# Neighbourhood attention with the meta keys in the right strip's unused column, and a new order of the splits at the up stage's border

## The chip, the cores and the metric

The kernel runs on one core of a Trainium2 chip. The metric is the device time of one execution in microseconds (us); the median of three runs before the change is 1512.63 us (1512.05 to 1513.26).

## The reference

One layer of an encoder on 16 meta tokens and 1024 real tokens of width 1024, in float32. The real tokens form a grid of 16 rows and 64 columns.

```
a = rms_norm(h, g)
q_na, k_na, v_na, q_hg, z_f, z_b, i_hg, g_hg, gate_na, gate_hg = split(a @ W_in)
A  = neighbourhood_attention(q_na, k_na, v_na, rpb) @ W_na      # 8 heads of 64
Bm = hgrn2(q_hg, z_f, z_b, i_hg, g_hg) @ W_hg                   # 4 heads of 128
h  = h + (sigmoid(gate_na) * A + sigmoid(gate_hg) * Bm) @ W_o
h  = h + square(relu(rms_norm(h) @ W_up)) @ W_down              # 4096 wide
out = rms_norm(h)[16:]
```

In the attention a query at row r, column c sees 8 rows and 16 columns (both clamped at the grid's borders; in the middle the columns c-8 to c+7) with a bias by relative place, and all 16 meta keys. One softmax runs over the 128 + 16 scores.

## The kernel before

**Precision.** Every large product is made of float32r matmuls: each operand is split into a high part (a rounding copy, on ACT) and a low part (a subtraction, on DVE), and three matmuls, high x high, high x low and low x high, are added up in PSUM (`mm3`, L121; `chain`, L913: twelve matmuls of 512 columns over four blocks of 128). Transposes are plain float32 matmuls with the identity.

**Stages in order of time.** Projections and the gated recurrence (to about 340 us); the attention, head pair by head pair (about 340 to 580); the gates, the two branch outputs, W_o; the up product; the down product. Where nothing is said, a planner orders the instructions of all engines by program order as priority and by a model of costs. Where `manual_schedule` is open for an engine, program order is its order.

**The attention** (L749 to L899), for each of four pairs of heads. The 64 columns are cut into 8 strips of 8 columns; a strip has 16 x 8 = 128 tokens. Queries stand in `QX`, keys in `KS` (high part) and `KL` (low part), each strip of keys followed by the 16 meta keys, SW = 144 columns in all. Inside a strip tokens run row by row, so that the evictions of the projections (`ev_k`, L790; `ev_vn`, L810) write runs. `mev_k` (L799) puts the meta keys behind all eight strips.

`scores` (L831): for one strip and one head two matmuls (high and low keys) over the strips left, centre and right with their meta columns: 432 columns inside, 288 at the two edges. DVE adds bias and mask from `NB` and takes the minimum (L844), ACT makes the exponential and its sum (L846), DVE takes the reciprocal (L847) and scales (L848). A mask lets the meta columns count only once, behind the centre strip.

`values` (L851): each of the m strips of probabilities is transposed (L859), and once more the 128 columns that end with the meta columns of the centre (L861), so that the 16 meta probabilities stand in the last 16 rows of that block. ACT and DVE split the block into PH and PL (L870, L871). After four strips come the products with V, whose blocks hold 64 columns of the high and 64 of the low part: first the meta block V[:, 8] against the four meta blocks of PH, 512 columns (L875), then for each strip of keys one matmul with PH (L882) and one of the high part with PL (L883), as wide as the strips of queries that see it, last V[:, 8] against PL, 512 columns (L884). V[:, 8] is zero but for its last 16 rows. V's nine blocks come out of nine transposes of `vT` (L821) and a split (L823, L824).

The steps run in the order: four strips of head 0, four of head 1, then the other half; `values` lags `scores` by two steps. While that goes on the planner lets PE stream the projections of the next pair. `NB` is built on POOL (L774) from a bias and a mask that SP loads.

**The border to the up product** (L1278 to L1506). The rows of h, 128 at a time in `hres[0..7]`, get their W_o product, are written to DRAM (`row_scale`, L1231, on ACT's queue), scaled (`scale_row`, L1242), transposed back into place (`turn_back`, L1271), and combined two by two into the variants of a seven-product (Strassen-like) scheme: `row_sums` (L1245, two subtractions on DVE, two on POOL) gives t1, t2, t3, t4 and b22, and `split_rows(v, j)` (L1287, `to_variant` L1258) splits one block of one variant: one ACT copy and one DVE subtraction (L1261, L1262). From L1462 to the loop's end the order of all engines is written out by hand. The list `todo` holds the splits that are still open. For the first three pairs of column blocks of w_up the products with b11 and b21 (`product_1`, `product_2`) are made ahead, while row 7 and the splits are being finished; their weights are split by `weights` (L1323, ACT L1328, DVE L1329). Then the loop over the pairs runs products 3 to 7 with s4, s2, s1, s3, a22, the split sums of w_up's blocks (`pair_sums`, L1371).

## Time and profile before

| what | value |
|---|---|
| median of three runs | 1512.63 us |
| the profiled execution | 1511.24 us |
| its span, first to last instruction | 1509.5 us |
| granted TensorE clock | 0.999 |
| PE busy | 1492.1 us |
| DVE, ACT, POOL busy | 1035.8, 665.0, 370.7 us |

The span is that of one profiled execution. A row of a group gives the line, the engine, the operation, the tiles as out<-in with the shapes and the count; behind the bar the busy time in us and the mean of one in ns; behind the second bar the idle time of the engine just ahead of them and what ended it. A PE row with 128*128 128x512 has 128 x 128 weights and 512 moving columns. PEld rows are the loads of the weights, which overlap PE. PE's durations are latencies of a pipeline: in a timeline, starts tell the pace.

### The profile page before, as it was taken

Reading aid. Unit: us, or ns where it says so; the run is one execution under the profiler, and the core shown is the slowest. Engines: PE = TensorE matmul, PEld = TensorE weight load, DVE = VectorE, ACT = ScalarE, POOL = GpSimd, SP = SyncE. Lnnn points to the kernel's source line nnn. Section 1 sums busy time; section 2 is a strip of 40 time slices with the busy share of each in tenths; the row PEclk is TensorE's granted clock in tenths of the full one; section 3 lists DMA queues with packets and bytes.
Section 4 is the critical chain, followed back from the end, with each engine's and each line's share of the span. In section 5 each row is a group of like instructions: output and inputs, shape, how many; then the busy total and the mean of one; then the engine's idle time right before and its main releaser. Section 6 shows DMA issues by size and latency. Waiting matters only on the chain.

```text
span 1509.5 us, 23492 instructions
## 1 busy us (share of the span) xinstructions
PE 1492.1 (99%) x9200; PEld 1250.8 (83%) x9200; DVE 1035.8 (69%) x1622; ACT 665.0 (44%) x1185; POOL 370.7 (25%) x349
## 2 busy tenths in 40 slices
PE   9999999999999999999999999999999999999998
PEld 8888888888888888888888878888888888888886
DVE  7876666656786796675585478777777445877876
ACT  7131313135565576343133355555555534334444
POOL 3313131324414400110000131344444200231242
PEclk9999999999999999999999999999999999999999
DMA  4211011114212237444655124544444676563224
GB/s 170 59 30 57 29 50 37 44 30 132 87 63 95 98 91 259 140 152 168 223 169 209 42 91 167 168 154 154 154 154 153 203 252 234 189 233 112 96 84 154
DMA packets 142592, 195.62 MB, mean 130 GB/s; under 512 B 8192, under 2 KB 90368, under 8 KB 142480
## 3 DMA queue, kind: packets, MB, share of 16 engines
q1 hardware_dynamic: 133072, 172.34, 34.8%
q10 hardware_dynamic: 7232, 14.44, 2.5%
q0 software_dynamic: 2176, 7.34, 1.3%
q8 instruction: 72, 1.18, 0.3%
q14 instruction: 40, 0.33, 0.1%
HBM read 139.56 MB, written 54.53 MB: 129 GB/s over the span
## 4 chain that ended last, share of the span: by engine, by line
PE 92%; DVE 4%; issue 2%; ACT 2%; POOL 0%; DMA 0%; POOLq 0%; ACTq 0%; DVEq 0%
PE mm L122 11%; PE mm L123 11%; PE mm L124 11%; PE mm L1541 5%; PE pa L1541 5%; PE pb L918 4%; PE pb L919 4%; PE pb L920 4%; PE pb L1541 4%; PE pc L1541 4%; PE pc L920 3%; PE pc L919 3%; PE pc L918 3%; PE pa L920 2%; PE pa L919 2%
## 5 line engine op out<-in xcount | busy, mean ns | idle before, releaser
L122 PE MATMUL mm<-aT,hi 128*128 128x512 f32 (+2 forms) x600 | 213.9, 357 | 0.0
L123 PE MATMUL mm<-aT,hi 128*128 128x512 f32 (+2 forms) x600 | 211.9, 353 | 0.0
L124 PE MATMUL mm<-aT,lo 128*128 128x512 f32 (+2 forms) x600 | 211.7, 353 | 0.0
L96 ACT CAST dh<-ur 128x1024 fp32r<-128x1024 f32 x54 | 56.9, 1054 | 166.5 <-issue 91.1
L97 DVE TENSOR_TENSOR dl<-ur,dh 128x1024 fp32r<-128x1024 f32 x54 | 70.0, 1297 | 87.0 <-ACT dh L96 85.2
L122 PEld LDWEIGHTS mm<-aT,hi 128*128 128x128 f32 x600 | 113.2, 189 | 12.6
L124 PEld LDWEIGHTS mm<-aT,lo 128*128 128x128 f32 x600 | 113.2, 189 | 12.3
L123 PEld LDWEIGHTS mm<-aT,hi 128*128 128x128 f32 x600 | 113.3, 189 | 12.0
L1333 ACT ACTIVATE uv<-uv 128x512 f32<-128x512 f32 x48 | 30.4, 633 | 82.3 <-DVE uv L1441 52.8
L1329 DVE TENSOR_TENSOR wl<-sx,wh 128x512 fp32r<-128x512 f32 x70 | 62.1, 897 | 3.6 <-ACT wh L1328 3.6
L1329 DVE TENSOR_TENSOR wl<-raw,wh 128x512 fp32r<-128x512 f32 x50 | 39.0, 783 | 36.4 <-ACT wh L1328 36.3
L112 ACT CAST hi<-raw 128x1024 fp32r<-128x1024 f32 x26 | 27.3, 1052 | 77.1 <-PE mm L123 71.3
L1328 ACT CAST wh<-sx 128x512 fp32r<-128x512 f32 x70 | 42.3, 620 | 38.5 <-PE pc L919 24.8
L1631 POOL TENSOR_TENSOR w<-w,tt 128x512 f32<-128x512 f32 x16 | 24.3, 1521 | 132.3 <-DVE tt L1630 111.1
L844 DVE CUSTOM_DVE_ANT_0 pr<-nsc,NB 128x432 f32<-128x432 f32 (+1 forms) x64 | 35.3, 560 | 30.2 <-issue 22.9
L300 POOL TENSOR_TENSOR Y<-X,TN 128x512 f32<-128x512 f32 x20 | 34.2, 1711 | 83.4 <-DVE X L297 83.4
L122 PE MATMUL mm<-wh,mT 128*128 128x512 f32 x128 | 50.2, 392 | 0.0
L123 PE MATMUL mm<-wl,mT 128*128 128x512 f32 x128 | 50.1, 391 | 0.0
L124 PE MATMUL mm<-o,lo 128*128 128x512 f32 x128 | 49.9, 390 | 0.1
L918 PE MATMUL pb<-nt,wh 128*128 128x512 f32 x128 | 49.9, 390 | 0.0
L124 PE MATMUL mm<-wh,mT 128*128 128x512 f32 x128 | 49.9, 390 | 0.0
L123 PE MATMUL mm<-o,hi 128*128 128x512 f32 x128 | 49.8, 389 | 0.0
(432 smaller groups left out, 4425.3 us busy)
## 6 DMA issues: line engine op xcount, KB each, us to landing
raw<-in_w_in SPq DMA_DIRECT2D x56, 512.0 KB, 3.9
ur<-usp SPq DMA_DIRECT2D x54, 512.0 KB, 3.6
raw<-in_w_up SPq DMA_DIRECT2D x16, 1024.0 KB, 6.2
usp<-us SPq DMA_DIRECT2D x60, 256.0 KB, 2.4
sg<-gsp SPq DMA_DIRECT2D x16, 512.0 KB, 5.1
w<-in_w_dn SPq DMA_DIRECT2D x16, 512.0 KB, 5.0
usp<-uv SPq DMA_DIRECT2D x30, 256.0 KB, 2.3
gsp<-gv ACTq DMA_DIRECT2D x24, 256.0 KB, 2.4
```

What stands on the lines that cost most here:

```text
L96: act.copy(hi, src)
L97: dve.tensor_tensor(lo, src, hi.bitcast(F32), op=ALU.subtract)
L122: pe.matmul(ps, lh, rh, start=first, stop=False)
L123: pe.matmul(ps, lh, rl, start=False, stop=False)
L124: pe.matmul(ps, ll, rh, start=False, stop=last)
L844: dve.tensor_tensor_reduce(out=pr[:, :w], in0=sc[:, :w], in1=NB[:, i, o:o + w], scale=1.0, scalar=3.0e38, op0=ALU.add, op1=ALU.min, accum_ ...
L918: pe.matmul(ps, lhs[0][:, c], rhs[0][:, k], start=first and k == 0, stop=False, skip_group_check=True)
L919: pe.matmul(ps, lhs[0][:, c], rhs[1][:, k], start=False, stop=False, skip_group_check=True)
L920: pe.matmul(ps, lhs[1][:, c], rhs[0][:, k], start=False, stop=k == 3, skip_group_check=True)
L1328: act.copy(v(hi), src)
L1329: dve.tensor_tensor(v(lo), src, v(hi).bitcast(F32), op=ALU.subtract)
L1541: pe.matmul(ps, a[n == 2][:, q, j * P:(j + 1) * P], b[n == 1][:, q], start=first and n == 0, stop=last and n == 2, skip_group_check=True)
```

## The change

**Attention.** The tokens of a key strip run column by column, with the 16 meta keys ahead of them. Seen from its query strip, the last column of the right strip never lies in the window; so the right strip is read from its start, 16 meta keys and seven columns, 128 in all, and an inner strip's scores are 3 x 128 columns: two matmuls of 256 and two of 128. The two edge strips keep two matmuls of 288. The probabilities are transposed in three blocks of 128 everywhere. V gets 14 blocks: eight whole strips, and six (strips 2 to 7) that begin with the meta values; they take 14 transposes in four batches. The 512-column meta products are gone; a right strip is a matmul of its own with its own V block, and only each half's edge strip has a meta product left, over 16 rows. Bias and mask are laid out accordingly on the host.

**Border.** Four of the row tiles (`hres` 2, 6, 3, 7) move to a pool of their own, `hrb`, whose slots later hold w_up's split weights in place of the pool `upr`. The first half of the third pair's weights is split ahead of row 7's scaling, from `upf`, which gets two buffers. Row 7's spill goes to SP's queue. The last `row_sums` runs on DVE alone. The splits of t3 and t4 for blocks 2 and 3 are put off: two to the place ahead of pair 2's product 2, one behind the next weights, one behind the first product 6; the remaining ones move between the products.

```diff
-        vT = npl.tile([P, 9, P], F32, name="vT")
-        V = npr.tile([P, 9, 2, P], F32R, name="Vn")
+        def key_strips(t, p0, t0, n):
+
+            a = t[p0:p0 + 64, :, NM:].rearrange("p s (c r) -> p s r c", r=ROWS)
+            return a[:, :, t0 // 64:(t0 + n) // 64]
...
-                    act.copy(strips(KS[i], 64 * i, t0, n), grid(ps, 64 * i))
+                    act.copy(key_strips(KS[i], 64 * i, t0, n), grid(ps, 64 * i))
...
-                    dve.tensor_tensor(strips(KL[i], b, t0, n), grid(ps, b),
-                                      strips(KS[i], b, t0, n).bitcast(F32), op=ALU.subtract)
-                    act.copy(strips(KS[i], 64 - b, t0, n), strips(KS[i], b, t0, n).bitcast(F32))
+                    dve.tensor_tensor(key_strips(KL[i], b, t0, n), grid(ps, b),
+                                      key_strips(KS[i], b, t0, n).bitcast(F32), op=ALU.subtract)
+                    act.copy(key_strips(KS[i], 64 - b, t0, n), key_strips(KS[i], b, t0, n).bitcast(F32))
...
             def mev_vn(ps):
-                act.copy(vT[:, 8, P - NM:], ps)
+                act.copy(vT[:, :, :NM], ps.unsqueeze(1).broadcast_to([P, 8, NM]))
             proj(C_VN + p * P, ev_vn, mev_vn)
-            for b in (0, 4, 8):
+            whole = [vT[:, j, NM:] for j in range(8)] + [vT[:, j, :P] for j in range(2, 8)]
+            for b in range(0, len(whole), 4):
...
             def scores(s, i):
-                js = [j for j in (s - 1, s, s + 1) if 0 <= j < 8]
-                w = len(js) * SW
-                o = 432 if s == 0 else 720 if s == 7 else 0
-                sc = bank("s", "nsc").rearrange("p a b -> p (a b)")
-                ksl = KS[i][:, js[0]:js[-1] + 1].rearrange("p s c -> p (s c)")
-                kll = KL[i][:, js[0]:js[-1] + 1].rearrange("p s c -> p (s c)")
-                pe.matmul(sc[:, :w], QX[i][:, s], ksl, start=True, stop=False)
-                pe.matmul(sc[:, :w], QX[i][:, s], kll, start=False, stop=True)
-                pr = npr.tile([P, 432], F32, tag="pr", name="pr", bufs=5)
+                sc = bank("s", "nsc")
+                scf = sc.rearrange("p a b -> p (a b)")
+                if 0 < s < 7:
+                    w, o = 3 * P, 0
+                    runs = [(sc[:, :2], [K[i][:, s - 1:s + 1, NM:] for K in (KS, KL)]),
+                            (sc[:, 2], [K[i][:, s + 1, :P] for K in (KS, KL)])]
+                else:
+                    w, o = 2 * SW, 3 * P + (2 * SW if s else 0)
+                    j = max(s - 1, 0)
+                    runs = [(scf[:, :w], [K[i][:, j:j + 2].rearrange("p s c -> p (s c)") for K in (KS, KL)])]
+                for dst, (ks, kl) in runs:
+                    pe.matmul(dst, QX[i][:, s], ks, start=True, stop=False)
+                    pe.matmul(dst, QX[i][:, s], kl, start=False, stop=True)
+                sc = scf
+                pr = npr.tile([P, 3 * P], F32, tag="pr", name="pr", bufs=5)
...
-                    po[i] = [npr.tile([P, 22, P], F32R, tag=f"PT{q}", name=f"PT{q}") for q in range(2)]
+                    po[i] = [npr.tile([P, 19, P], F32R, tag=f"PT{q}", name=f"PT{q}") for q in range(2)]
...
-                for k in range(m):
-                    pe.transpose(pt[:, k], pr[:, k * SW:k * SW + P], ident)
-                cen = js.index(s)
-                pe.transpose(pt[:, m], pr[:, cen * SW + NM:cen * SW + NM + P], ident)
-
-                b0 = 3 * (js[0] - 4 * g) + e + 3
-                if s < 7:
-                    runs = [(0, m + 1, b0)]
-                else:
-                    runs = [(0, m, b0), (m, 1, 4 * e + 9)]
-                for k, n, b in runs:
-                    hi = PH[:, b:b + 3 * n - 2:3]
-                    act.copy(hi, pt[:, k:k + n])
-                    dve.tensor_tensor(PL[:, b:b + 3 * n - 2:3], pt[:, k:k + n], hi.bitcast(F32), op=ALU.subtract)
+                for k, c in enumerate((0, P, 2 * P) if 0 < s < 7 else (NM, SW + NM, SW)):
+                    pe.transpose(pt[:, k], pr[:, c:c + P], ident)
+                b0 = 3 * (max(s - 1, 0) - 4 * g) + e + 3
+                hi = PH[:, b0:b0 + 7:3]
+                act.copy(hi, pt[:, :3])
+                dve.tensor_tensor(PL[:, b0:b0 + 7:3], pt[:, :3], hi.bitcast(F32), op=ALU.subtract)
...
-                pe.matmul(ov, V[:, 8, i], PH[:, 9:22:4], start=True, stop=False)
-                for a in range(-1, 5):
+
+                def add(v, n, b, e0, ne, start=False, stop=False):
+                    pe.matmul(ov[:, e0:e0 + ne], V[:n, v, i], PH[:n, b:b + ne], start=start, stop=False,
+                              skip_group_check=True)
+                    pe.matmul(ov[:64, e0:e0 + ne], V[:n, v, i, :64], PL[:n, b:b + ne], start=False, stop=stop,
+                              skip_group_check=True)
+
+                for a in (0, 2, -1, 1, 3, 4):
                     j = 4 * g + a
-                    if 0 <= j < 8:
-                        es = [q for q in range(4) if abs(a - q) <= 1]
-                        e0, ne = es[0], len(es)
-                        b = 3 * a + e0 + 3
-                        pe.matmul(ov[:, e0:e0 + ne], V[:, j, i], PH[:, b:b + ne], start=False, stop=False)
-                        pe.matmul(ov[:64, e0:e0 + ne], V[:, j, i, :64], PL[:, b:b + ne], start=False, stop=False)
-                pe.matmul(ov, V[:, 8, i], PL[:, 9:22:4], start=False, stop=True)
+                    if not 0 <= j < 8:
+                        continue
+                    es = [q for q in range(4) if abs(a - q) <= 1]
+                    if a > 0 and 4 * g + a - 1 > 0:
+                        add(6 + j, P, 4 * a + 2, a - 1, 1)
+                        es.remove(a - 1)
+                    if es:
+                        add(j, P, 3 * a + es[0] + 3, es[0], len(es), start=a == 0)
+                add(8, NM, *((18, 3) if g else (9, 0)), 1, stop=True)
...
-    hress = ExitStack()
+    hresb, hress = ExitStack(), ExitStack()
+    hrb = hresb.enter_context(tc.tile_pool(name="hrb", bufs=1, side="right", reuse_waits="tile"))
     hrp = hress.enter_context(tc.tile_pool(name="hrp", bufs=1, side="right", reuse_waits="tile"))
     hres = [None] * 8
-    for i in (2, 6, 3, 7, 0, 4, 1, 5):
+    for i in (2, 6, 3, 7):
+        hres[i] = hrb.tile([P, D], F32, tag="hb", name=f"hres{i}", bufs=4)
+    for i in (0, 4, 1, 5):
         hres[i] = hrp.tile([P, D], F32, name=f"hres{i}")
...
-        junk = rowp.tile([P, D], F32, tag="junk", name="junk", bufs=2)
-        act.dma_start(hsp[i], hres[i])
+        junk = rowp.tile([P, D], F32, tag="junk", name="junk")
+        (sp if i == 7 else act).dma_start(hsp[i], hres[i])
...
-        pool.tensor_tensor(b12, b22, b12, op=ALU.subtract)
-        pool.tensor_tensor(b21, b21, t2, op=ALU.subtract)
+        eng = dve if j == 3 else pool
+        eng.tensor_tensor(b12, b22, b12, op=ALU.subtract)
+        eng.tensor_tensor(b21, b21, t2, op=ALU.subtract)
...
-        hi, lo = (a_tile(pool_ or w_pools[-1], t, F32R, 1 if pool_ else 4) for t in ("wh", "wl"))
+            pool_ = w_pools[-1]
+        if pool_ is hrb:
+            w = hrb.tile([P, D], F32R, tag="hb", name="wb", bufs=4)
+            hi, lo = w[:, :TH], w[:, TH:]
+        else:
+            hi, lo = (a_tile(pool_, t, F32R, 4 if pool_ is upw else 2) for t in ("wh", "wl"))
...
-        rs7 = row_scale(7)
-        todo = [(v, j) for j in range(3) for v in ("t1", "t3", "t4")]
-        todo += [(v, 3) for v in ("b22", "t2", "t1", "t3", "t4")]
+        todo = [(v, j) for j in range(2) for v in ("t1", "t3", "t4")] + [("t1", 2)]
+        todo += [(v, 3) for v in ("b22", "t2", "t1")] + [("t3", 2), ("t4", 2), ("t3", 3), ("t4", 3)]
 
         def splits(n=1):
             for _ in range(n):
                 split_rows(*todo.pop(0))
 
         def last_row(k):
-            if k == 0:
-                scale_row(7, rs7)
-            elif k == 3:
+            if k == 3:
                 turn_back(hres[7][:, :TH], dve)
                 turn_back(hres[7][:, TH:], act)
-                nB.append(row_sums(3))
             else:
-                splits()
-
-        product_1(pairs[0], first_w[0][0], lambda k: splits(k > 0))
+                splits(k > 0)
+
+        def third_weights(q):
+            first_w.setdefault(2, []).append(weights(first_raw[2][:, 4 * q:4 * q + 4], upf))
+
+        splits()
+        rs7 = row_scale(7)
+        third_weights(0)
+        splits()
+        scale_row(7, rs7)
+        splits()
+        product_1(pairs[0], first_w[0][0])
         product_1(pairs[1], first_w[1][0], last_row)
-        first_weights(2, 0)
+        nB.append(row_sums(3))
         splits(2)
-        product_1(pairs[2], first_w[2][0], lambda k: splits(), "mm")
-        product_2(pairs[0], first_w[0][1], lambda k: (splits(k < 3), last_first_weights(k)))
+        third_weights(1)
+        product_1(pairs[2], first_w[2][0], lambda k: splits(k > 0), "mm")
+        product_2(pairs[0], first_w[0][1])
         rows_.close()
         hress.close()
 
         rawp = ups.enter_context(tc.tile_pool(name="rawp", bufs=1, side="right", reuse_waits="tile"))
-        upr = ups.enter_context(tc.tile_pool(name="upr", bufs=1, side="right", reuse_waits="tile"))
         load_pair(0)
         load_pair(1)
         pair_sums(pairs[0])
         product_2(pairs[1], first_w[1][1])
         next_weights(-1, "s4", "s2")
+        splits(2)
         product_2(pairs[2], first_w[2][1])
         early_w.close()
         psum_pools(pc=2, pb=2, pa=2)
         upb = ups.enter_context(tc.tile_pool(name="upb", bufs=1, reuse_waits="tile"))
-        w_pools.insert(0, upr)
+        w_pools.insert(0, hrb)
         next_weights(-1, "s1", "s3", "a22")
+        splits()
         for m, q in enumerate(pairs):
             if m + 2 < NP + 2:
                 load_pair(m + 2)
             (product_3 if q.early else product_1)(q)
             if m == 0:
                 product_6(q)
+                splits()
```

70 lines of the change are left out of this document (38 added, 32 removed).

## Prediction

> **What bounds the kernel now.** I read the page first: who is busy, and what the chain that ended last consists of.
>
> ```profile
> PE 1492.1 (99%) x9200; PEld 1250.8 (83%) x9200; DVE 1035.8 (69%) x1622; ACT 665.0 (44%) x1185; POOL 370.7 (25%) x349
> PE 92%; DVE 4%; issue 2%; ACT 2%; POOL 0%; DMA 0%; POOLq 0%; ACTq 0%; DVEq 0%
> ```
>
> TensorE (PE) is busy 99% of the span and makes up 92% of the chain. So time is won by giving PE less to stream, or by closing one of its few gaps. Both halves of the change aim at PE. Then the windows, for who else is close to full in the attention stage (columns: length, PE, PEld, DVE, ACT, POOL busy, clock, DMA):
>
> ```profile
> 400.00:420.00 20.00, 20.00 (x117) 17.61 (x116) 7.39 (x16) 9.52 (x21) 12.22 (x14) 1.00 0.49 152
> 480.00:500.00 20.00, 20.00 (x122) 16.85 (x121) 19.38 (x59) 13.10 (x32) 0.00 (x0) 1.00 0.00 0
> ```
>
> The stage alternates: in the softmax stretches (480 to 500) PE is full, because projections of the next head pair fill it, and DVE is nearly full as well (19.38 of 20). Between them (400 to 420) PE streams projections alone and DVE does 7.39. The granted clock is 1.00. So PE is the limit, with DVE right behind it for part of the time.
>
> A PE row's duration is a latency; what an instruction costs is the distance to the next start. The PE timeline of one value product gives the prices:
>
> ```profile
> 372.22 0.36 PE L838 MATMUL nsc<-KS,QX 128*128 128x432 f32 x1
> 372.42 0.36 PE L839 MATMUL nsc<-KL,QX 128*128 128x432 f32 x1
> 372.62 0.40 PE L124 MATMUL mm<-aT,lo 128*128 128x512 f32 x1
> 372.85 0.39 PE L122 MATMUL mm<-aT,hi 128*128 128x512 f32 x1
> ...
> 373.22 0.48 PE L875 MATMUL pov<-PT,Vn 128*128 128x512 f32 x1
> 373.53 0.28 PE L882 MATMUL pov<-PT,Vn 128*128 128x256 f32 x1
> 373.65 0.28 PE L883 MATMUL pov<-PT,Vn 128*64 128x256 f32 x1
> 373.77 0.33 PE L882 MATMUL pov<-PT,Vn 128*128 128x384 f32 x1
> 373.94 0.34 PE L883 MATMUL pov<-PT,Vn 128*64 128x384 f32 x1
> ...
> 374.69 0.22 PE L882 MATMUL pov<-PT,Vn 128*128 128x128 f32 x1
> 374.75 0.22 PE L883 MATMUL pov<-PT,Vn 128*64 128x128 f32 x1
> 374.81 0.45 PE L884 MATMUL pov<-PT,Vn 128*128 128x512 f32 x1
> 375.10 0.27 PE L861 MATMUL ppt<-ident,pr 128*128 128x128 f32 x1
> 375.21 0.49 PE L859 MATMUL ppt<-ident,pr 128*128 128x128 f32 x3
> ```
>
> By differences of starts: 512 columns 0.23 us, 432 columns 0.20, 384 0.17, 256 0.12, 128 0.06 (374.69 to 374.75 to 374.81), a plain float32 transpose 0.11 (375.10 to 375.21). The first matmul behind transposes costs 0.31 instead of 0.23, the last one ahead of them 0.29: 0.14 for going in and out. One value group takes 375.10 - 373.22 = 1.88.
>
> **The change in the attention.** The counts:
>
> ```profile
> L859 PE MATMUL ppt<-ident,pr 128*128 128x128 f32 x176 | 30.7, 276 | 1.3 <-DVE rc L847 0.5 <-DVE pr L848 0.5
> L838 PE MATMUL nsc<-KS,QX 128*128 128x432 f32 x48 | 19.6, 409 | 0.0
> L861 PE MATMUL ppt<-ident,pr 128*128 128x128 f32 x64 | 17.4, 273 | 0.0
> L821 PEld LDWEIGHTS vpt<-ident,vT 128*128 128x128 f32 x36 | 4.0, 140 | 1.1 <-ACT vT L812 0.7 <-issue 0.2
> ```
>
> - Probability transposes: 176 + 64 = 240 now, three for each of 64 strips and heads afterwards = 192. 48 x 0.11 = -5.3.
> - Scores: 48 inner strips go from two matmuls of 432 columns (0.40) to two of 256 and two of 128 (0.24 + 0.12 = 0.36). -1.9. The 16 edge strips stay at 288.
> - Value products, 16 groups (4 pairs, 2 heads, 2 halves). The two 512-column meta products go. In the first half the new adds have widths 2, 1, 2, 3, 1, 1, 1, 1 blocks of 128, each with the high and the low probabilities: 2 x (2 x 0.12 + 0.17 + 5 x 0.06) = 1.42. In the second half 2, 1, 2, 1, 1, 2, 1, 1, 1: 2 x (3 x 0.12 + 6 x 0.06) = 1.44. With 0.14 for in and out about 1.57, against 1.88: 16 x 0.31 = -5.0.
> - Transposes of V: 14 blocks a pair for 9, 20 x 0.11 = +2.2, and a fourth batch a pair, 4 x 0.14 = +0.6.
>
> Sum on PE: -5.3 - 1.9 - 5.0 + 2.8 = -9.4. PE is full here, so this is time, if no other engine takes its place. DVE's own account:
>
> ```profile
> L871 DVE TENSOR_TENSOR PT<-ppt,PT 128x512 fp32r<-128x512 f32 x48 | 32.6, 680 | 0.4
> L871 DVE TENSOR_TENSOR PT<-ppt,PT 128x384 fp32r<-128x384 f32 x8 | 4.5, 557 | 0.2
> L824 DVE TENSOR_TENSOR Vn<-vpt,Vn 128x512 fp32r<-128x512 f32 (+1 forms) x12 | 6.3, 553 | 0.1
> ```
>
> The split of the probabilities gets shorter, 48 x (0.680 - 0.557) = -5.9, the split of V longer, 6.3 / 36 = 0.175 a block, 20 blocks = +3.5; the softmax steps on 384 in place of 432 columns shrink too, by an amount I leave out. So DVE loses at least 2.4 us. ACT, at 13.10 of 20 in the full stretch, has room.
>
> What the change adds is a layout. Keys and values are now stored column by column in a strip, so the evictions of K and V (both halves, and KS's copy to the other half) write, and partly read, every 16th element, 64 bytes apart. Before they wrote runs. The trace has one scattered operation, the multiplication at line 421: its first level (the row with T) touches lone elements, the others (TN) pairs of neighbours or repeats.
>
> ```profile
> L421 DVE TENSOR_TENSOR QQ<-QQ,TN x48: 664/685/1536, 65.8 to 316.0; 128x512 f32<-128x512 f32 x48
> L421 DVE TENSOR_TENSOR QQ<-QQ,T x8: 1109/1116/1872, 58.8 to 287.1; 128x512 f32<-128x512 f32 x8
> L795 DVE TENSOR_TENSOR KL<-mm,KS 64x256 fp32r<-64x256 f32 (+1 forms) x24 | 12.3, 511 | 3.8 <-ACT KS L792 3.3
> L797 ACT CAST KS<-KS 64x256 fp32r<-64x256 f32 (+1 forms) x24 | 11.4, 476 | 0.3
> L812 ACT COPY vT<-mm 64x256 f32<-64x256 f32 (+1 forms) x24 | 10.5, 438 | 0.3
> L792 ACT CAST KS<-mm 64x256 fp32r<-64x256 f32 (+1 forms) x24 | 10.5, 438 | 4.0 <-PE mm L124 2.2 <-DVE KL L806 1.4
> ```
>
> Lone elements cost 1116 ns for 512 where the others cost 685: a factor of 1.63. On the four eviction groups, 12.3 + 11.4 + 10.5 + 10.5 = 44.7 us, that would be +28.2 of busy time at most, and nothing at least. The Trainium skill ("SBUF — State Buffer", Specifications (TRN2)) has a rule that speaks against the change: lines are 16 bytes, and full rate wants two hits on a line. The trace agrees with it in the two rows of line 421. Most of such a stretch would be covered: K's evictions fall into the projection stretches, where DVE has 20 - 7.39 = 12.6 us free and V's projection runs before the first scores. Uncovered is the last V piece: the transposes of V already wait for ACT's copy of vT (0.7 us in the L821 row), so no slack is there. A stretch of half of L812's 10.5 x 0.63 would cost 3.3 over four pairs. If PE has other matmuls ahead, it costs 0. The waits are nearer to 0, as the planner puts projections between; I take +1.0.
>
> The bound of the 128-column price: 0.06 in the rows above, but there at most two of them follow each other, each with its own weights; afterwards up to eight do. The nearest dearer row is the transpose, 0.11, which also changes its weights every time. I take 0.06, being the same kind of instruction. "TensorE: Matmul & The Clock Gate" of the Trainium skill (Back-to-back issue gap) gives about 81 ns for a sustained stream of 128-column matmuls with their weight loads; the 60 ns of this trace are below it, and by the page the sum would be an estimated 5.7 us worse.
>
> **The change at the border.** PE's waits, all of the kernel's over 1 us but the first, stand here; then DVE and POOL at that place:
>
> ```profile
> PE mm L920 <- DVE wl L1329: 1.3, 1, 1.3
> PE pt L1268 <- DVE hres L1243: 1.2, 1, 1.2
> PE mm L918 <- ACT wh L1328: 1.2, 1, 1.2
> ```
>
> ```profile
> 888.67 1.90 DVE L1262 TENSOR_TENSOR nt<-hres,nt 128x512 fp32r<-128x512 f32 x3 [2.10 <-ACT nt L1261]
> 890.48 1.28 DVE L1243 SCALAR_TENSOR_TENSOR hres<-hres,rs,g 128x1024 f32<-128x1024 f32 x1
> ...
> 895.01 1.77 DVE L1329 TENSOR_TENSOR wl<-sx,wh 128x512 fp32r<-128x512 f32 x1
> 896.70 3.58 DVE L1262 TENSOR_TENSOR nt<-hres,nt 128x512 fp32r<-128x512 f32 x4
> ...
> 907.18 1.29 DVE L1329 TENSOR_TENSOR wl<-sx,wh 128x512 fp32r<-128x512 f32 x2 [0.76 <-ACT wh L1328]
> ```
>
> ```profile
> 894.44 1.79 POOL L1251 TENSOR_TENSOR hres<-hres 128x512 f32<-128x512 f32 x1 [5.40 <-DVE hres L1249]
> ```
>
> PE waits 1.2 for row 7's scaling, then 1.2 and 1.3 for the third block's weights, 3.7 in all. A split costs 1.29 / 2 = 0.65 on DVE. The change casts the first half of the third weights ahead of that scaling, from a buffer of its own: the last two waits go. The scaling itself: DVE idles 2.10 before 888.67; now one split fits into that, and then the third weights and one split stand ahead of the scaling in place of three splits. It starts about one split earlier: 1.2 becomes 0.6. Row 7's spill moves from ACT's queue to SP's, where nothing but the later loads of w_up stand behind it; the scaling overwrites that row and must wait for the spill, but DVE arrives no earlier than that.
>
> What is late next: PE reaches the first product with s4 some 3 us sooner, and DVE must have split s4 by then. Ahead of s4 DVE has four splits less (10 for 14, -2.6), two subtractions more, taken from POOL (+1.3), and no longer shares the time with POOL: while POOL subtracts, one wl takes 1.77 and four splits 3.58, 1.1 and 1.0 over 0.65 each (-2.1). That is 3.4 earlier, about when PE arrives; I leave 0.6 for a new wait. The four splits put off are due at t3's and t4's products, at least three chains of 12 x 0.23 on, 8 us. Border: -3.7 + 0.6 + 0.6 = -2.5, with -3.7 and 0 as ends. Sharing the row tiles' slots with weights (hrb) makes s1 and a22 wait for those splits on ACT, behind which product copies of ACT stand; the splits come a full chain earlier, so I cost that at nothing (0.6 if a cast waits for one split).
>
> **Sum.** -9.4 + 1.0 - 2.5 = -10.9. The profiled execution took 1511.24 us (span 1509.5 and 1.7 around it): 1500.3. The median of the runs is 1.4 above the profiled one: 1501.7.
>
> **Rivals.**
> - *DVE becomes the bound of the softmax stretches.* For: 19.38 of 20. Against: what DVE has left over slips into the next stretch, where it does 7.39. The stage would gain DVE's 2.4 alone: 1512.6 - 2.4 - 2.5 = 1507.7. Chance 0.12.
> - *The border's wait comes back at s4 or at a22.* For: DVE has no gap from 888.67 on. Against: the count above. 1501.7 + 2.5 = 1504.2. Chance 0.10.
> - *Single-block matmuls run at the pace of weight loads.* There are 22 x 8 in the value products and 96 in the scores, 272. For: eight in a row is new. Against: 0.06 between different weights. At 0.11 it is 272 x 0.05 = +13.6: 1515.3; halfway, +6.8: 1508.5. The rule of "TensorE: Matmul & The Clock Gate" in the Trainium skill lies near that halfway point. Chance 0.08.
> - *Slower: the scattered evictions land on PE.* Place: the projections' banks and the transposes of V, which wait for ACT and DVE. Price: up to 28.2, so 1501.7 - 1.0 + 28.2 = 1528.9. It decides from 11.9 of the 28.2 on, 42%. For: the factor 1.63 is in the trace, for DVE. Against: half of DVE and ACT is free where K is evicted. Chance 0.07.
>
> **How the numbers follow.** Forecast 1501.7 with 0.60 (its own range 1497 to 1504.5); 0.03 is left for a larger gain from the planner's new order. Measured differences under 0.2%, 3 us, can't be told from none, so no change is 1509.6 to 1515.7. The range 1497 to 1508.5 takes in the first two rivals and the halfway point of the third. Faster: 0.60 + 0.12 + 0.10 + 0.03 and half of the third, 0.89. Same: 0.04, the other half. Slower: 0.07.
>
> **What would show it.** Right: 192 probability transposes; a value group of about 1.57 from its first to its last start; PE's waits for L1243 and L1329 at 0.6 or gone; the stretch from the first scores to the last value group 2.4 us a pair shorter, PE still full. Wrong: PE waiting for vT or for K's evictions; the copies of K and V at 1.6 times their time and late; singles over 0.06 apart; a wait of 2 us or more ahead of the first s4 product.

## The result, and the profile after

The prediction was wrong: the change makes the kernel slower. Median 1540.21 us (5 runs, 1539.31 to 1541.11) against 1512.63 us before (5 runs, 1512.05 to 1515.79); ratio 1.0171, 95% interval 1.0159 to 1.0183. The profiled execution took 1540.25 us, its span 1538.5. Forecast were -10.9 us, measured are +27.6.

The page of after, engines and chain:

```profile
PE 1502.6 (98%) x9348; PEld 1260.0 (82%) x9348; DVE 1037.8 (67%) x1620; ACT 683.4 (44%) x1181; POOL 363.4 (24%) x346
PE 86%; DVE 6%; ACT 4%; issue 2%; DMA 1%; POOL 1%; SPq 0%; ACTq 0%; POOLq 0%; DVEq 0%
```

PE's share of the span falls by a point, of the chain by six. Where it happened, the starts of PE's rows tell: the first scores of the four pairs start at 360.9, 417.9, 473.8 and 530.2 us before, at 362.1, 426.0, 490.2 and 553.2 after, and the gates' first product with `at` behind the last pair at 601.3 and 633.2. So each pair takes 63 to 64 us in place of 56 to 57, the last one 80.0 in place of 71.1. From that product to the up border's first the traces agree (284.4 us in both). From the border's first product to the first one with s4 it is 21.7 before and 17.7 after; of the 4.0, the second landmark's start to the end of the span gives 1.1 back. So the loss is in the attention: 21.8 us in the first three pairs, 8.9 in the last; another 1.2 stand ahead of the first scores.

One pair, the second, cut at its last value group: the stretch with softmax, and the projections alone behind it (columns: length, PE, PEld, DVE, ACT, POOL busy, clock, DMA). First before, then after:

```profile
417.84:453.84 36.00, 35.88 (x223) 30.21 (x222) 34.08 (x97) 27.17 (x65) 6.10 (x5) 1.00 0.14 44
453.84:473.75 19.91, 19.91 (x122) 17.96 (x121) 7.52 (x12) 7.48 (x18) 15.13 (x16) 1.00 0.47 153
```

```profile
426.00:462.00 36.00, 30.84 (x212) 26.25 (x210) 30.33 (x92) 23.22 (x57) 2.46 (x4) 0.95 0.14 43
462.00:490.15 28.15, 28.15 (x169) 25.23 (x170) 11.86 (x16) 16.00 (x25) 16.65 (x16) 1.00 0.34 109
```

This pair's stretch has kept its length to the hundredth, but PE is no longer full in it (30.84 of 36.00), and VectorE isn't either (30.33). The block behind it has grown by 8.2 us. (The granted clock of 0.95 isn't the cause: the next pair's stretch has 1.00 and takes 34.8 us, with 29.46 of PE busy.) The same two windows with the projection products alone, before and after:

```profile
417.84:453.84 36.00, 18.91 (x76) 1.00 0.14 44
453.84:473.75 19.91, 19.53 (x118) 1.00 0.47 153
```

```profile
426.00:462.00 36.00, 10.01 (x26) 0.95 0.14 43
462.00:490.15 28.15, 28.02 (x167) 1.00 0.34 109
```

Of this pair's 192 projection products 74 stood beside softmax before, and 25 after (the windows' edges count one or two of the neighbours). The other 49 follow alone. The third pair has the same numbers, the first 77 and 31, the last, where the gates' products are the fill, 72 and 30. That is the loss: PE works less in the stretch, waits there, and has the projections still to do. What it waits for, over the whole kernel:

```profile
PE ppt L872 <- DVE PT L876: 8.1, 7, 1.4
PE pov L882 <- DVE OT L901: 4.6, 6, 0.9
PE vpt L829 <- ACT vT L819: 3.7, 4, 0.9
PE pov L882 <- ACT PT L875: 1.6, 8, 0.3
```

Before, no row of PE's waits in the attention came to 1 us in total. The transposes now wait for VectorE to free their bank, the value groups for the sum that frees theirs. The row of vT is the one that the prediction named as a sign against it, and it is the third. PE is idle for 35.9 us of the span in place of 17.4, 18.5 more of the 29.0. The rest of the loss stands in the page as busy time (1502.6 for 1492.1): a row's duration is a latency, 0.22 us for a 128-column product where the next one starts 0.06 later, so that a PE at 98% can still be short of work.

### The profile page after: what moved, and what is told of

Read it like the earlier page. It is cut to its first block, busy times and chain, and to the rows that moved or that the text cites. A ratio compares the mean times of both kernels' runs of the same rounds, so it can differ in the third digit from the quotient of the medians.

```text
span 1538.5 us, 23805 instructions
## 1 busy us (share of the span) xinstructions
PE 1502.6 (98%) x9348; PEld 1260.0 (82%) x9348; DVE 1037.8 (67%) x1620; ACT 683.4 (44%) x1181; POOL 363.4 (24%) x346
## 4 chain that ended last, share of the span: by engine, by line
PE 86%; DVE 6%; ACT 4%; issue 2%; DMA 1%; POOL 1%; SPq 0%; ACTq 0%; POOLq 0%; DVEq 0%
PE mm L123 11%; PE mm L124 11%; PE mm L125 11%; PE mm L1567 5%; PE pa L1567 4%; PE pb L931 4%; PE pb L932 4%; PE pb L933 4%; PE pb L1567 4%; PE pc L1567 4%; PE pc L933 3%; PE pc L932 3%; PE pc L931 3%; PE pa L932 2%; PE pa L933 2%
## 5 line engine op out<-in xcount | busy, mean ns | idle before, releaser
L858 DVE CUSTOM_DVE_ANT_0 pr<-nsc,NB 128x384 f32<-128x384 f32 (+1 forms) x64 | 33.1, 519 | 25.8 <-issue 19.3
L123 PE MATMUL mm<-o,hi 128*128 128x512 f32 x128 | 49.8, 389 | 0.0
L124 PE MATMUL mm<-o,hi 128*128 128x512 f32 x128 | 49.8, 389 | 0.0
L1567 PE MATMUL mm<-dl,dh 128*128 128x512 f32 x124 | 48.6, 392 | 0.3 <-DVE dl L98 0.2
L1567 PE MATMUL mm<-dh,dl 128*128 128x512 f32 x124 | 48.3, 390 | 0.0
L1567 PE MATMUL mm<-dh 128*128 128x512 f32 x124 | 48.1, 390 | 0.0
```

The costliest lines, as they stand in the source:

```text
L123: pe.matmul(ps, lh, rh, start=first, stop=False)
L124: pe.matmul(ps, lh, rl, start=False, stop=False)
L858: dve.tensor_tensor_reduce(out=pr[:, :w], in0=sc[:, :w], in1=NB[:, i, o:o + w], scale=1.0, scalar=3.0e38, op0=ALU.add, op1=ALU.min, accum_ ...
L1567: pe.matmul(ps, a[n == 2][:, q, j * P:(j + 1) * P], b[n == 1][:, q], start=first and n == 0, stop=last and n == 2, skip_group_check=True)
```

## The experiments

Theory A, from these rows: the planner put fewer projections between the softmax steps, and so the work that the change takes from PE turns into waiting. Its rival B is the fourth rival of the prediction: the scattered evictions hold everything up. C: VectorE bounds the stretch. All ratios are to the kernel before, timed beside the run on the same chip. Its median there lay between 1513.6 and 1514.5, 1.0 to 1.9 above the 1512.63 that stood beside the changed kernel. So what a run gains over the changed kernel's 1540.21 is 1.0 to 1.9 larger when each is taken against its own neighbour.

| run | median, us | ratio (95%) |
|---|---|---|
| border_alone | 1510.72 | 0.9977 (0.9968 to 0.9987) |
| in_runs | 1536.13 | 1.0145 (1.0130 to 1.0160) |
| hand72 | 1535.86 | 1.0140 (1.0125 to 1.0156) |
| hand24 | 1549.20 | 1.0229 (1.0212 to 1.0246) |
| one_pair_scores | 1531.28 | 1.0109 (1.0091 to 1.0127) |
| full_hand | 1542.64 | 1.0185 (1.0169 to 1.0201) |
| trail_after | 1538.21 | 1.0160 (1.0144 to 1.0175) |
| trail_before | 1537.25 | 1.0152 (1.0135 to 1.0169) |
| order_of_before | 1519.21 | 1.0028 (1.0017 to 1.0040) |
| order_and_runs | 1515.89 | 1.0013 (1.0004 to 1.0022) |
| split_scores | 1528.82 | 1.0095 (1.0078 to 1.0112) |
| wider_scores | 1533.07 | 1.0127 (1.0112 to 1.0142) |

**The border alone.** The edits from the row tiles on (hrb, the order of splits and casts); the attention and its inputs stay as before.

> The border's edit alone, the attention as before. Two theories of the 28 us that the whole change lost. A (few projections between the softmax steps): the loss lies in the attention alone, and the border gives what the two traces differ by between the up border's first product and the first product against s4 (21.70 us before, 17.74 after, of which about 2.9 us lasts to the end): 1509.7 us, faster than the kernel before. B (scattered key and value evictions) expects the same. If the border were part of the loss, it would come out at 1512.6 or more.

Measured: 3.4 us faster than before (1514.12 beside it). It is the only one of the twelve that is faster than the kernel before. PE's waits between 850 and 950 us:

```profile
PE pb L918 <- DVE uv L1435: 0.5, 1, 0.5
PE pt L1272 <- DVE hres L1246: 0.4, 1, 0.4
```

Of the three waits that made 3.7, those for the third weights are gone, and row 7's is down from 1.2 to 0.4.

**The evictions in runs.**

```
-            a = t[p0:p0 + 64, :, NM:].rearrange("p s (c r) -> p s r c", r=ROWS)
+            a = t[p0:p0 + 64, :, NM:].rearrange("p s (r c) -> p s r c", c=8)
```

> The changed kernel, but the evictions of K and V write runs of 8 elements, as before, in place of single elements 64 bytes apart (same count and sizes; the keys then stand in another order than the bias and the mask, so the output is not the reference's). B (the stretched evictions hold ACT and VectorE up, and TensorE with them) expects most of the loss back: 1509 to 1518 us. A (TensorE has too few projection products between the softmax steps, wherever the evictions go) expects only TensorE's visible waits for vT's evictions back, 3.7 us and up to 2 more where VectorE is freed: 1533 to 1538 us.

Measured: 1536.13, so 4.1 us of 27.6 (5.6 against its own neighbour). The planner gave this run the order of the changed kernel: the attention's operations on PE, ACT and VectorE follow each other as there, and the second pair has as few projections beside softmax:

```profile
425.20:459.10 33.90, 9.47 (x26) 1.00 0.15 46
459.10:487.20 28.10, 28.00 (x167) 1.00 0.34 109
```

So the difference is the price of the evictions alone, and they are not what moved the projections. B falls as the main cause. It isn't nothing, though. Rows of before and of after between 420 and 560 us (mean ns of one in the last column but one):

```profile
L812 ACT COPY vT<-mm 64x512 f32<-64x512 f32 x5 | 2.9, 581 | 0.1
L795 DVE TENSOR_TENSOR KL<-mm,KS 64x512 fp32r<-64x512 f32 x4 | 2.8, 689 | 0.1
```

```profile
L819 ACT COPY vT<-mm 64x512 f32<-64x512 f32 x6 | 6.3, 1044 | 0.1
L802 DVE TENSOR_TENSOR KL<-mm,KS 64x512 fp32r<-64x512 f32 x5 | 5.5, 1098 | 2.0 <-ACT KS L799 1.9
```

Writing every 16th element costs ACT a factor of 1.80. VectorE's factor is 1.59; its row also reads one operand (KS) in that way.

**PE's order by hand, with many and with few projections.** PE's order of pairs 0 to 2 is the order of the program text; before each transposes' step stand some products of the next pair's Q and K. hand24 differs only in these numbers (NAHEAD = 1: one Q piece is computed ahead).

```
+        NAHEAD, LAG = 3, 4
+        EARLY, LATE = [2, 3, 3, 3, 2, 3, 3, 3, 2, 3, 3, 3, 2, 3, 3, 3], 6
...
+        by_hand.enter_context(tc.manual_schedule(engines={pe.engine}))
...
+                fill(EARLY[n])
+                if group:
+                    group = group()
+                if len(pend) > LAG:
+                    group = values(*pend.pop(0))
```

> The changed kernel with TensorE's order in the attention written by hand for pairs 0 to 2: 72 projection products of the next pair (its two Q pieces and the first K piece, as many as the order of before has) stand between the softmax steps, some 3 to a step, and the value group of four strips follows the next step's scores. Evictions still scattered. A expects the saving that was forecast, about 1500 us, up to 1510 if the hand order has waits of its own. B expects no gain, 1530 or more, since the evictions are as long as in the changed kernel. A third theory, C (VectorE's own work bounds the stretch whatever TensorE does), expects 1525 or more too.

> The same hand order with only 24 projection products (one Q piece) between the softmax steps, as few as the changed kernel has; the other 48 of each of three pairs follow alone. A expects the loss back: 48 x 3 products at 0.23 us for the Q piece and 0.12 for the K piece, 5.5 + 2.9 us a pair, no longer hidden, so 20 to 30 us above the run with 72, 1525 to 1540 us. B and C expect the two to be within 5 us of each other.

Measured: 1535.86 and 1549.20. The direction is A's: 48 products a pair moved out of the stretch cost 13.3 us. The size isn't: A wanted 20 to 30, and the run with 72 was to reach 1510. It came out where B (1530 or more) and C (1525 or more) had it. Against both stands the difference of the two runs, which they expected to be 5 us at most. The stretch has grown in the projections' place. Windows of hand72, then hand24:

```profile
426.75:468.05 41.30, 36.47 (x258) 31.92 (x257) 35.21 (x97) 27.76 (x64) 7.44 (x9) 1.00 0.16 50
468.05:488.15 20.10, 20.10 (x122) 18.13 (x123) 7.32 (x11) 11.89 (x19) 10.44 (x11) 1.00 0.40 126
```

```profile
431.90:468.90 37.00, 29.91 (x210) 24.78 (x208) 30.99 (x93) 23.34 (x57) 5.43 (x6) 1.00 0.13 42
468.90:497.40 28.50, 28.50 (x171) 25.55 (x172) 10.99 (x15) 15.98 (x26) 12.46 (x14) 1.00 0.34 108
```

The block behind is as short as before's (20.10 for 19.91), but 41.30 are spent on the stretch. Waits of PE in that pair of hand72:

```profile
PE ppt L921 <- DVE PT L925: 1.9, 1, 1.9
PE vpt L878 <- ACT vT L868: 1.9, 1, 1.9
PE pov L936 <- DVE PT L925: 0.9, 4, 0.4
```

So the number of projections isn't enough. That they have to stand where PE would wait is argued here, and C is still open.

**One pair of scores in place of two.**

```
-                    runs = [(sc[:, :2], [K[i][:, s - 1:s + 1, NM:] for K in (KS, KL)]),
-                            (sc[:, 2], [K[i][:, s + 1, :P] for K in (KS, KL)])]
+                    runs = [(scf[:, :w], [K[i][:, s - 1:s + 2].rearrange("p s c -> p (s c)")[:, NM:NM + w] for K in (KS, KL)])]
```

> The changed kernel, the order left to the planner, but the inner strips' scores are one pair of products over 384 neighbouring columns in place of a pair of 256 and a pair of 128 (the third block is then not the one with the meta keys, so the output is not the reference's). Work on every engine stays the same within 0.02 us a step; TensorE only gets 24 instructions fewer a pair. D (the planner holds the 128-column products for dearer than they are, or counts instructions, sees TensorE full and moves projections out of the softmax stretch) expects more projections in the stretch and with them some of the loss back: by what 48 more of them a pair were worth in the hand order (13.3 us) about 18 of 48, 5 us, so 1532 to 1536 us. If the fill is set by something else (buffers, ACT and VectorE): 1539 to 1541.

Measured: 1531.28, 8.9 us back where about 5 were expected. The planner put 46 to 48 projections into each stretch, for 25 to 31.

**All three engines by hand.** The order of PE, ACT and VectorE is written out for all four pairs, with the gates' products as fill of the last. In the first order VectorE's softmax step follows the scores of the same step, in the second those of the step before it (the second's lines):

```
+                if n < len(steps):
+                    pr, soft = scores(*steps[n])
+                    pend.append((*steps[n], pr))
+                if ready:
+                    scales.append(ready())
```

> The changed kernel with the order of TensorE, ACT and VectorE in the attention written by hand: the same 72 projection products of the next pair in the softmax stretch, also for the last pair (48 of the gates' first products), and beside them the first three strips' scores go into the V projection's last piece, so that 24 more lie beside softmax; transposes follow their scores four steps later, and a strip group's value products one step after its last transposes. The first hand order left TensorE 6.9 us a pair of waits (vT 2.1, a transposes' bank 2.2, value groups 2.4) over 54.5 of work. A (the loss is TensorE's waiting, and its work did fall as forecast) expects about 55 to 57 us a pair, so 1500 to 1512 us. C (VectorE's own 42 us a pair bound the stretch wherever the projections stand) expects 1525 or more.

> The changed kernel with a second full hand order of the attention: as the first, but VectorE's and ACT's softmax work trails TensorE's scores by a step, so that the engines don't wait for each other in turn (in the first order a step took 3.1 us where no engine had more than 2.4 of work), and the splits of the next weights stand behind the first softmax steps. A (TensorE's waits are the loss): 55 to 58 us a pair in place of 63.6, so 1500 to 1515 us. C (VectorE bounds it): no better than the first full order, 1535 or more.

> The attention of before (432-column scores, four blocks of probabilities) with the border of after, in the very same hand order as the run beside it. This compares the two attentions without the planner. A: the saving of TensorE work shows, this is 5 to 10 us slower than the changed attention in the same order (forecast 9.4, less what VectorE takes back). If the changed attention is slower for what it is (its evictions, its many products) and not for the order it was given, this one is the faster by 10 us or more.

Measured: 1542.64, 1538.21 and 1537.25. My orders were poor: a pair took 63.6 us in the first and 61.2 in the second, with 96 products in the stretch. A missed by over 20 us, and C's 1535 or more came true. But one comparison can be made: in one and the same order the attention of after and that of before differ by 1 us, where planned they differ by 29 (after against border_alone). Windows of trail_after and trail_before, one pair each:

```profile
419.50:465.80 46.30, 42.43 (x283) 36.29 (x282) 33.15 (x94) 26.93 (x64) 5.05 (x6) 1.00 0.24 76
```

```profile
420.80:467.30 46.50, 41.67 (x246) 35.34 (x245) 34.79 (x94) 26.24 (x64) 5.62 (x6) 1.00 0.23 73
```

This points to the order. That the attention of after has less work doesn't show, and with PE waiting in both (42.43 of 46.30, 41.67 of 46.50) it could hardly show. It brought theory E: the two attentions are nearly the same work, and the order that they are given decides.

**The order of before.** The three engines' orders are read off the kernel before, one letter for an operation (for PE: S scores, T transposes of probabilities, V of V, G a value group, m a projection product), and the operations of after are issued in them:

```
+        PE_ORDER = (
...
+            "VmmmTmmTmmmSTmmmTmSmmTGTSSmTmmmmmTmmmTGSTSSmmmmmmTmmTmSmmmmSmmGTTmmmmmmmmmmmmTmmmmmTmmmmmm"
...
```

> The changed kernel, with its own operations, evictions and border, but TensorE, ACT and VectorE take them in the attention in the order that the kernel before has: step by step, the same number of projection products between the same steps (72 to 77 a pair beside softmax), the same place of each eviction, softmax operation and weight split; a strip group's 16 or 18 value products stand where before has its 12, the two further V transposes beside the ninth. For the last pair the gates' products are left for the planner to place. Theory E (the two attentions are nearly the same work, and the order they are given decides): the run's two fully hand-ordered attentions took the same time, 1538.2 and 1537.3, 27 us over the planner's order of before; so this comes out near the run with the border alone (1510.7), less what TensorE work fell in the traces by (5.45 to 4.23 us of probability transposes, 7.6 to 7.25 of value products, 6.7 to 6.8 of scores, 0.8 to 1.4 of V transposes a pair: 1.0 us, 4 in all): 1503 to 1515. If the changed attention's own evictions or products set the pace in any order: 1530 or more.

> The run beside it with the evictions of K and V written in runs of 8 elements (keys then in another order than bias and mask, so the output is not the reference's): what the scattered evictions cost where TensorE is kept full. In the planner's order of after they cost 4 us. E expects 0 to 4 us less than the run beside it.

Measured: 1519.21 and 1515.89. So 21.0 of the 27.6 us were the order, with every operation of the change in place. The second pair in order_of_before, its windows:

```profile
418.95:457.45 38.50, 36.73 (x258) 31.71 (x257) 32.62 (x96) 27.54 (x64) 3.60 (x4) 1.00 0.13 42
457.45:477.55 20.10, 20.10 (x124) 18.09 (x123) 9.13 (x12) 11.73 (x19) 15.23 (x16) 1.00 0.50 152
```

The block is back at 20.10 and PE nearly full, 36.73 of 38.50. This decides against C: VectorE does the work of after, 32.62 + 9.13 us here for 30.33 + 11.86 there, and the pair takes 58.6 us for 64.2. The run still ends 4 us above the upper end that E gave, and 8.5 above border_alone. Of that, 4.7 are the last pair (75.8 us from its first scores to the gates' first product with `at`, for 71.1), where the gates' products were left to the planner, and 3.3 are the scattered evictions, by the run beside it, which has the same last pair (76.0).

Nor does PE's work fall by the forecast amount where PE is kept full. A whole value group of this run, with no wait in it, says why:

```profile
375.22 0.37 PE L930 MATMUL pov<-PT,Vn 128*128 128x256 f32 x1
375.42 0.28 PE L932 MATMUL pov<-PT,Vn 128*64 128x256 f32 x1
375.54 0.22 PE L930 MATMUL pov<-PT,Vn 128*128 128x128 f32 x1
375.60 0.22 PE L932 MATMUL pov<-PT,Vn 128*64 128x128 f32 x1
375.65 0.33 PE L930 MATMUL pov<-PT,Vn 128*128 128x256 f32 x1
375.83 0.28 PE L932 MATMUL pov<-PT,Vn 128*64 128x256 f32 x1
...
376.30 0.22 PE L930 MATMUL pov<-PT,Vn 128*128 128x128 f32 x1
376.36 0.22 PE L932 MATMUL pov<-PT,Vn 128*64 128x128 f32 x1
376.42 0.27 PE L930 MATMUL pov<-PT,Vn 128*128 128x128 f32 x1
376.53 0.23 PE L932 MATMUL pov<-PT,Vn 128*64 128x128 f32 x1
376.59 0.27 PE L930 MATMUL pov<-PT,Vn 128*128 128x128 f32 x1
376.70 0.22 PE L932 MATMUL pov<-PT,Vn 128*64 128x128 f32 x1
376.85 0.32 PE L930 MATMUL pov<-PT,Vn 16*128 16x128 f32 x1
377.01 0.22 PE L932 MATMUL pov<-PT,Vn 16*64 16x128 f32 x1
377.16 0.44 PE L886 MATMUL ppt<-ident,pr 128*128 128x128 f32 x2
```

377.16 - 375.22 = 1.94, where the prediction had 1.57 and before took 1.88. Two things cost more than was priced.

- A high product (`128*128`) behind a one-block low one (`128*64`) takes 0.05 to 0.06 more than behind a wider one: 0.11 for 0.06 (376.42 to 376.53, 376.59 to 376.70), and with 256 columns 0.18 for 0.12 (375.65 to 375.83). Together 0.16 in this group.
- The two products over 16 rows take 0.16 and 0.15 for 0.06, and the one in front of them 0.15: 0.28 in this group.

The 0.06 that the prediction allowed for going over to the transposes behind the group isn't spent, so the group is 0.37 over the forecast and not 0.44. Both costs stand in all 16 groups of the run (medians 0.111 and 0.171; 0.165, 0.147 and 0.152). The eight 128-row single products take 0.66 together, 0.083 each, and 0.073 without the one in front of the 16 rows. What makes these products dear is not shown.

**Is it the 128-column form?** The attention of before with its 432 columns cut in two, and the changed kernel with its 128 columns widened to 256:

```
+                for c in ((slice(0, 304), slice(304, w)) if w > 288 else (slice(0, w),)):
+                    pe.matmul(sc[:, c], QX[i][:, s], ksl[:, c], start=True, stop=False)
+                    pe.matmul(sc[:, c], QX[i][:, s], kll[:, c], start=False, stop=True)
```

```
-                            (sc[:, 2], [K[i][:, s + 1, :P] for K in (KS, KL)])]
+                            (sc[:, 2:], [K[i][:, s:s + 2, :P] for K in (KS, KL)])]
```

The second starts a strip early, so that the third block holds other keys than the reference's; its expectation has that wrong.

> The run with the border alone (attention of before), but each inner strip's scores, a pair of products of 432 columns, are two pairs of 304 and 128: same numbers, same VectorE and ACT work, no scattered evictions, four blocks of probabilities. TensorE's own work rises by some 0.05 us a step, 2.6 us in all (two of 304 at 0.14, one of 128 at 0.06 and one at 0.11, against two of 0.195). F (the planner, that sees 128-column products as far dearer than the chip takes for them, thins out the projections beside softmax): this alone costs as the change did, in part: fewer than 30 in place of 44 projection products before the first pair's last scores, some 30 more of them a pair behind, and 1520 to 1530 us. Without an effect on the order: 1510.7 + 2.6 = 1513.

> The changed kernel, but the inner strips' second pair of scores computes 256 columns in place of 128 (the further block is read by nobody and the bank is free; for the last columns it reads what stands in the next strip; the result is the reference's). TensorE's work rises by 24 products a pair from about 0.085 to 0.12, 0.8 us a pair, 3 in all; the number of instructions is the same. F (it is the 128-column form that the planner holds for dear, dearer than 256 columns) expects the fill to rise all the same, and the kernel that computes more to be faster by 3 to 7 us: 1533 to 1537. If the number of instructions were what the planner counts, or the order did not matter: 1540 to 1543.

Measured: 1528.82 and 1533.07, both inside what F expected (27 products, for 44, before the first pair's last scores in split_scores). Projection products of one pair in split_scores, then in wider_scores:

```profile
421.80:458.90 37.10, 15.16 (x48) 1.00 0.14 43
458.90:482.10 23.20, 22.93 (x145) 1.00 0.43 131
```

```profile
423.00:460.00 37.00, 14.21 (x43) 1.00 0.13 42
460.00:484.30 24.30, 24.18 (x150) 1.00 0.40 126
```

Cutting one matmul in two, which costs PE some 2.6 us, loses 18 us over border_alone: 47 products beside softmax in place of 74. Computing more than is needed gains 7.1 us over the change: 42 in place of 25. The count of instructions is the same in wider_scores and after, so the count alone isn't what the planner went by. What it went by is in no trace: that 128 columns weigh more with it than 256 fits these two runs and one_pair_scores, but it is argued from three plans, not shown.

## Why the prediction was wrong, step by step

**The step that failed** is "PE is full here, so this is time, if no other engine takes its place", with "the planner puts projections between" as what was to keep PE full. The prediction took the order as given and let the operations shrink in it. Its one mention of a new order is a chance of 0.03 for a larger gain. But the order is planned anew for the new operations, and it came out with 25 of a pair's projections beside softmax in place of 74 (31 for 77 in the first pair). The sign that the prediction named, a stretch 2.4 us shorter a pair with PE full, failed: to the start of the last value product the stretches of the four pairs are 37.0, 36.0, 34.8 and 35.9 us long, for 37.7, 36.0, 36.6 and 38.2, so 0 to 2.3 shorter, PE isn't full in them, and the blocks behind them grew by 8. With the order of before on the changed operations, 21.0 us went away.

**The price of PE's work** was the second error. The probability transposes came as forecast: 192, in groups of three that take 0.246 where four took 0.355, 48 x 0.109 = -5.2. The transposes of V take 1.42 us a pair for 0.82, +2.4 for the forecast +2.8. But the value groups take 1.94 for 1.89 (medians of the groups without a wait, order_of_before and before), 16 x 0.05 = +0.8 in place of -5.0, and the inner scores that stand between projections 0.408 for 0.390, 48 x 0.018 = +0.9 in place of -1.9. Sum -1.1 in place of -9.4. The larger part of what a value group costs over its 1.57 is the product over 16 rows, 0.28, which the forecast priced like any other single. The third rival had the mechanism of the smaller part: singles in a row cost more, and neither 0.06 nor 0.11 but both by turns. The page "TensorE: Matmul & The Clock Gate" of the Trainium skill (Back-to-back issue gap) gives 81 ns for such a stream; the eight singles' mean of 0.083 lies near it, but takes in the 0.15 ahead of the 16 rows, and the other seven take 0.073.

The trace of before held the dear case already. A 256-column high product behind a one-block low one takes 0.17 there, the low one after it 0.12:

```profile
445.03 0.23 PE L883 MATMUL pov<-PT,Vn 128*64 128x128 f32 x1
445.09 0.33 PE L882 MATMUL pov<-PT,Vn 128*128 128x256 f32 x1
445.26 0.28 PE L883 MATMUL pov<-PT,Vn 128*64 128x256 f32 x1
445.38 0.33 PE L882 MATMUL pov<-PT,Vn 128*128 128x384 f32 x1
```

The group that the prediction shows has it too. The prediction read the 0.29 of the last 512-column product as the price of going over to the transposes. But in all eight groups with 0.28 to 0.29 that product stands behind a one-block low one; in the four that go over to transposes from behind a 256-column one it takes 0.23 (390.23 to 390.46 in one). The two neighbours at 0.06 that the forecast rested on stood behind a wider product, and they are the cheap case.

**The border** was right, in mechanism too: -2.5 forecast, with -3.7 as the better end, and -3.4 measured alone. The profile after shows row 7's wait at 0.3 and no other wait above 0.4 at the border, so the 0.6 that was kept for a new wait was not needed, and the second rival falls.

**The scattered evictions** were sized at +1.0 with 0 to 3.3 as bounds; they cost 4.1 to 5.6 in the planner's order and 3.3 in that of before. The factor 1.63 from line 421, a row of VectorE, came out as 1.59 on VectorE and 1.80 on ACT. These rows side with the Trainium skill's rule ("SBUF — State Buffer", Specifications (TRN2)) that full rate wants two hits on a line of 16 bytes, as line 421 did. But as what makes the kernel slower, rival 4, the evictions are refuted: that it named the right side is luck, its mechanism is 4 to 6 us of 27.6.

**VectorE as the bound**, rival 1, isn't what came. Its room in the stretch was 36.00 - 34.08 before, so PE's saving could not have shortened the stretch by much, unless VectorE's did; no run tests that by itself. In after it is no bound: 30.33 of 36.00, and PE 30.84. Neither is full; they wait for each other in the order that they were given. What exactly keeps the stretch at 35 to 37 us with 25 products as with 47 stays open.

The sum again: 1501.7 forecast; +8.3 for PE's prices, -0.9 for the border and +2.3 for the evictions (3.3 for 1.0) give 1511.4. Another 4.7 for the last pair's order and 3.1 that are not told apart (waits left in the other three pairs, and 1.7 by which the kernel before itself took longer beside this run) give the 1519.2 of order_of_before, and the planner's order 21.0 more.

## What to carry to other kernels

Where a planner places the work, the price of an edit is the new order as much as the new instructions: a full engine stays full only if the same filler is still placed in the same waits. So count the filler (here the projection products beside softmax) and not only the work taken away; and when a change breaks one wide matmul into narrow ones, try it with the old order before judging it. Price a narrow matmul from a whole group with its neighbours, not from its cheapest pair of starts, and take no price for a form that stands nowhere in the trace (here 16 rows) from one that does.

## What the hardware showed that I had not expected

- A write of every 16th float32 (64 bytes apart) costs ACT's copy of 64x512 1044 ns for 581; VectorE's subtraction, which also reads one operand so, takes 1098 for 689.
- A one-block (128 columns) product takes 0.06 us behind a wider one, and 0.06 and 0.11 by turns in a row, where stationary operands of 128 and 64 columns alternate. The 0.05 more go with standing behind a one-block low product, whatever the width: 256 columns 0.17 for 0.12, 512 columns 0.29 for 0.23.
- A product over 16 rows, an eighth of the data, takes 0.15 to 0.17, more than one over 128 rows, and the one in front of it 0.15.
